# Gate and up of a SwiGLU FFN as one stage in emission order: where the sums of x, the first unit's preparation and the last unit's products stand

## The chip, the cores and the metric

The kernel runs on one core of one Trainium2 chip. The metric is the device time of one execution in microseconds (us). A core has five engines with a queue of instructions each: TensorE (PE) for matmuls, with its weight loads shown apart as PEld, VectorE (DVE), ScalarE (ACT), GpSimd (POOL) and SyncE (SP), which here only issues DMAs. An engine takes its instructions in the order of its queue; between engines, semaphores hold an instruction until its inputs are there and its output's memory is free.

## The reference

One decoder block on x of 512 tokens by 1024 features, in float32: a half FFN, a mixer (retention and a convolution, gated), and another half FFN, each with a residual and a layer norm behind it. The change touches only the gate and up products of the two FFNs.

```python
def swiglu_ffn(h, w_gate, w_up, w_down):
    return (jax.nn.silu(h @ w_gate) * (h @ w_up)) @ w_down

    for l in range(DEPTH):
        x = layer_norm(alpha * x + 0.5 * swiglu_ffn(x, ffn1_w_gate[l], ffn1_w_up[l], ffn1_w_down[l]), ...)
        m = hybrid_mixer(x, ...)
        x = layer_norm(alpha * x + m, ln2_g[l], ln2_b[l])
        x = layer_norm(alpha * x + 0.5 * swiglu_ffn(x, ffn2_w_gate[l], ffn2_w_up[l], ffn2_w_down[l]), ...)
```

w_gate and w_up are 1024 x 2816, w_down is 2816 x 1024.

## The kernel before

**Numbers in two parts.** Every operand of a matmul is split into a rounded part and a rest (`split`: a cast on ACT writes the "hi" tile, a subtraction on DVE writes the "lo" tile), and each product is three matmuls: hi·hi, hi·lo, lo·hi. `xh` and `xl` are the two parts of x, features on the partitions.

**Units.** The 2816 columns of gate and up are 22 units of 128 columns (`NF`). A unit is one DMA of 1 MB into a `raw` tile (two buffers), holding the unit's gate and up weights. The first `N_STD` units (2 in FFN1, 3 in FFN2) are done plainly: `feat_proj` for gate and for up, 24 matmuls of 512 columns each, then `silu_times`: silu of gate on ACT (tile `sg`), times up on DVE, into `h`. In FFN1 the first of them is `first_unit`, which loads the weights and x in pieces; in FFN2 two are started by the mixer's last layer norm (`token_proj` with `ahead`), their weight parts lying in tiles `z` of the mixer's pool "mix". The last of the plain units is called the late unit below; it goes through `load_unit`.

**Strassen units.** The other units (20 in FFN1, 19 in FFN2) compute gate and up of one unit as a 2 x 2 block product by a Strassen-Winograd scheme with seven products in place of eight. For x, `strassen_x` forms four sums once for each FFN: f3 = b12 - b22, f1 = b11 - b12, f2 = -f1 - b22, f4 = f2 + b21 (each 128 x 1024), and splits them into `th`, `tl` (called t3, t1, t2, t4). In FFN2 x exists only as xh and xl, so each term is two operations. For each unit, `strassen_w` gives named steps: `load` (DMA), `s13` (one DVE operation), `s24` (two, of which the second reads the first), four casts on ACT (`hi_a` for a12 and a11, `hi_b` for s1 and s3, `hi_c` for s2 and s4, `hi_d` for a22) and four subtractions on DVE (`lo_a` to `lo_d`).

**The loop** is `strassen_rows`, in a section (`tc.manual_schedule()`) in which each engine's queue keeps the order in which the code emits it. Everything outside of such a section is ordered by a scheduler. A product is 12 matmuls of 256 columns. The order of PE in iteration u is: a11·b11 into bank z; s3·t3 into bank y; the s4·b22 of the unit before, into its z; s2·t2 added to z; a12·b21 into bank w; a22·t4 added to y; s1·t1 added to z. Since banks are added to, copies are taken by ACT (`z1`, `y1`, `z2`) before the next product goes into the same bank; `g1` = z1 + w is gate's first half, z after s4·b22 its second half; the two halves of up are `row2` = y - z2 and y1 - z. The next unit's steps are laid between these with `do(...)`. For the last unit the loop runs one iteration more, in which only s4·b22 and the outputs are left.

**Before the loop**, the sums of x, the splits, the silus of the plain units and the first Strassen unit's steps are outside of the section, so the scheduler places them.

**Memory.** Pools are stacked. In before, `th`, `tl` and `sg` are in pool "gu", the sums (`tf`, and `xf`, x as loaded in FFN1) in a pool "xin" above it, closed before the loop, and the loop's tiles in pool "strassen", which takes the place of "xin". A pool that takes the place of closed ones waits for their last users; with `reuse_waits="tile"` each tile waits only for those that lay at its own addresses.

Of the kernel before, what the change touches and what calls it, by code (L numbers as in the profile page):

```python
# [52 lines left out]
def block_kernel(ctx, tc, ap, out):  # L53
# [48 lines left out]
    def strassen_x(pool, tmp, parts):  # L102

        b = {}
        for i in range(2):
            for j in range(2):
                sl = (slice(None), slice(i * KH, (i + 1) * KH), slice(j * HS, (j + 1) * HS))
                b[i, j] = [p[sl] for p in parts], (xh[sl], xl[sl])

        def total(first, *rest):  # L110

            f = tmp.tile([P, KH, HS], F32, name="tf", bufs=2)
            terms = [(p, op) for ps, op in rest for p in ps]
            acc = first
            for p, op in terms:
                nc.vector.tensor_tensor(f, acc, p, op=op)  # L116
                acc = f
            return f

        def pair(f):  # L120
            hi = pool.tile([P, KH, HS], F32R, name="th", bufs=4)
            lo = pool.tile([P, KH, HS], F32R, name="tl", bufs=4)
            split(hi, lo, f)
            return hi, lo

        (b11, b12, b21, b22) = (b[i][0] for i in ((0, 0), (0, 1), (1, 0), (1, 1)))
        f3 = total(b12[0], (b12[1:], ALU.add), (b22, ALU.subtract))
        t3 = pair(f3)
        f1 = total(b11[0], (b11[1:], ALU.add), (b12, ALU.subtract))
        t1 = pair(f1)  # L130
        f2 = tmp.tile([P, KH, HS], F32, name="tf", bufs=2)
        nc.vector.scalar_tensor_tensor(f2, f1, -1.0, b22[0], op0=ALU.mult, op1=ALU.subtract)
        for p in b22[1:]:
            nc.vector.tensor_tensor(f2, f2, p, op=ALU.subtract)
        t2 = pair(f2)
        f4 = total(f2, (b21, ALU.add))
        return {"b11": b[0, 0][1], "b21": b[1, 0][1], "b22": b[1, 1][1],
                "t1": t1, "t2": t2, "t3": t3, "t4": pair(f4)}

    def strassen_w(pool, src):  # L140
# [15 lines left out]
        def s13():  # L156
            s[13] = pool.tile([P, 2, 512], F32, name="s13")
            nc.vector.tensor_tensor(s[13], raw[:, 0:4:2], raw[:, 3:4].to_broadcast([P, 2, 512]), op=ALU.add)  # L158

        def s24():  # L160
            s[24] = pool.tile([P, 2, 512], F32, name="s24")
            nc.vector.tensor_tensor(s[24][:, 0], s[13][:, 0], raw[:, 2], op=ALU.add)
            nc.vector.tensor_tensor(s[24][:, 1], s[24][:, 0], raw[:, 1], op=ALU.add)
# [18 lines left out]
    def strassen_rows(pool, units, xs, row1_done, row2_done, unit_done):  # L182
# [19 lines left out]
        prep = strassen_w(pool, units[0])  # L202
        for step in ("load", "s13", "hi_a", "hi_b", "s24", "lo_a", "hi_c", "lo_b", "hi_d", "lo_c", "lo_d"):
            prep[step]()
        with tc.manual_schedule():
            prev = None
            for u in range(len(units) + 1):
                n = strassen_w(pool, units[u + 1]) if u + 1 < len(units) else None

                def do(*steps):  # L210
                    for step in steps:
                        if n:
                            n[step]()

                do("load")
                cur = None
                if u < len(units):
                    w = prep["w"]
                    cur = dict(z=bank()[:, :HS], y=bank()[:, :HS], w=bank()[:, :HS], ws=w)
                    product(cur["z"], w["a11"], xs["b11"], True)  # L220
                if prev:
                    prev["row2"] = row2_done(u - 1)
                    nc.vector.tensor_tensor(prev["row2"][:, HS:], prev["y1"], prev["z"], op=ALU.subtract)
                do("hi_a", "s13")
                if cur:
                    z1 = copy("z1", cur["z"])
                    product(cur["y"], w["s3"], xs["t3"], True)
                do("hi_b", "lo_a")
                if cur:
                    cur["y1"] = copy("y1", cur["y"])  # L230
                if prev:
                    product(prev["z"], prev["ws"]["s4"], xs["b22"], False)
                    row1_done(u - 1, 1, prev["z"])
                do("s24", "lo_b", "hi_c")
                if prev:

                    nc.vector.tensor_tensor(prev["row2"][:, :HS], prev["yd"], prev["z2"], op=ALU.subtract)
                    unit_done(u - 1)
                if cur:
                    product(cur["z"], w["s2"], xs["t2"], False)  # L240
                    cur["z2"] = copy("z2", cur["z"])
                do("hi_d", "lo_c")
                if cur:
                    product(cur["w"], w["a12"], xs["b21"], True)
                    g = small("g1")
                    nc.vector.tensor_tensor(g, z1, cur["w"], op=ALU.add)
                    row1_done(u, 0, g)
                do("lo_d")
                if cur:
                    product(cur["y"], w["a22"], xs["t4"], False)  # L250
                    cur["yd"] = cur["y"]
                    product(cur["z"], w["s1"], xs["t1"], False)
                prev, prep = cur, n
# [209 lines left out]
    def ffn(w_gu, w_dn, res, row, dst, n_std, begin, ahead):  # L463
        with ExitStack() as es:
# [6 lines left out]
            with ExitStack() as es2:  # L471
                gp = es2.enter_context(tc.tile_pool(name="gu", bufs=1))

                def silu_times(ft, ps):
                    sg = gp.tile([P, S], F32, name="sg", bufs=2)
                    nc.scalar.activation(sg, ps[0], AF.Silu)
                    nc.vector.tensor_tensor(h[ft], ps[1], sg, op=ALU.mult)

                with tc.tile_pool(name="xin", bufs=1) as xp:
                    started, parts = begin(xp)  # L480
                    for ft in range(len(started)):
                        silu_times(ft, started[ft])
                    late = [unit_proj(w_gu[ft]) for ft in range(len(started), n_std)]
                    xs = strassen_x(gp, xp, parts)
                    for ft in range(len(started), n_std):
                        silu_times(ft, late[ft - len(started)])
                sp = es2.enter_context(tc.tile_pool(name="strassen", bufs=1, reuse_waits="tile"))
                sgs, ups = {}, {}

                def gate(u, half, src):  # L490
                    if half == 0:
                        sgs[u] = gp.tile([P, S], F32, name="sg", bufs=2)
                    nc.scalar.activation(sgs[u][:, half * HS:(half + 1) * HS], src, AF.Silu)

                def up(u):
                    ups[u] = sp.tile([P, S], F32, name="up2", bufs=2)
# [5 lines left out]
                strassen_rows(sp, [w_gu[ft] for ft in range(n_std, NF)], xs, gate, up, both)  # L502
# [18 lines left out]
    def first_unit(gp):  # L521
# [4 lines left out]
        xf = gp.tile([P, KD, S], F32, name="xf")  # L526
# [6 lines left out]
        def first_x(k):  # L533
            nc.sync.dma_start(xf[:, k, :], ap["xT"][:, k, :])
            split(xh[:, k, :], xl[:, k, :], xf[:, k, :])
# [12 lines left out]
        return [ps0], [xf]  # L548

    w_in = ap["w_in"]  # L550
    qk_glu = ffn(ap["w1gu"], ap["w1dn"], ap["x"], 0, scratch1, N_STD[0], first_unit, (w_in[U_QK], w_in[U_L]))
# [271 lines left out]
    def started_units(gp):  # L823
        return started, [xh.bitcast(F32), xl.bitcast(F32)]

    ffn(ap["w2gu"], ap["w2dn"], scratch2, 4, out, N_STD[1], started_units, ())
# [84 lines left out]
```

## Time and profile before

| | us |
|---|---|
| median of 3 runs | 1401.92 |
| lowest and highest | 1400.29, 1402.74 |
| the profiled execution, its own time | 1402.5 |
| its span, from first to last instruction | 1400.1 |
| PE busy | 1377.9 |
| DVE busy | 992.3 |
| ACT busy | 598.3 |

The span is what the profiler sees of one execution; the execution's own time is 2.4 us longer. Times in the rows below are from the span's start. A matmul's busy time overlaps the next one's, so a pace is read from the starts. In a row, "L191" is line 191 of the kernel, "out<-in" its tiles by name, and a bracket at the end is the idle time before it and what ended it.

### The profile page before, as it was taken

How to read it: one execution, taken by the hardware profiler on the slowest of the kernel's cores; microseconds unless marked ns; L12 is line 12 of the kernel's file. 1: busy time of each engine (PE TensorE's matmuls, PEld its weight loads, DVE VectorE, ACT ScalarE, POOL GpSimd, SP SyncE). 2: the span in 40 equal slices, each digit the busy share in tenths (PEclk: the TensorE clock that was granted, in tenths of full speed). 3: DMA queues.
4: the chain of work that ended last, by engine and by line, in shares of the span. 5: the costliest groups of instructions: out<-in, count | busy, mean ns of one | idle time of the engine just before them, and what ended most of it. 6: DMA issues, size and time to landing. Idle time of an engine off the chain costs nothing.

```text
span 1400.1 us, 19305 instructions
## 1 busy us (share of the span) xinstructions
PE 1377.9 (98%) x7974; PEld 1219.1 (87%) x7974; DVE 992.3 (71%) x1410; ACT 598.3 (43%) x872; POOL 21.8 (2%) x36
## 2 busy tenths in 40 slices
PE   8999999999999999999999999999998999999997
PEld 6999999888988888888888888888887999998886
DVE  7878786335787786786788996645497787884336
ACT  6545554233434434445344422473234555553221
POOL 0000000000000000000000000000000000000000
PEclk9999999999999999999999999999998999999999
DMA  5332234324322232231222223222340323235221
GB/s 188 119 110 102 103 109 159 143 91 154 147 75 98 73 107 84 90 106 69 90 98 91 91 91 151 85 96 91 133 169 30 120 93 115 96 108 194 90 90 60
DMA packets 26006, 150.83 MB, mean 108 GB/s; under 512 B 2880, under 2 KB 3008, under 8 KB 10432
## 3 DMA queue, kind: packets, MB, share of 16 engines
q1 hardware_dynamic: 25920, 149.62, 29.7%
q8 instruction: 62, 1.02, 0.3%
q14 instruction: 24, 0.20, 0.0%
HBM read 143.32 MB, written 6.29 MB: 107 GB/s over the span
## 4 chain that ended last, share of the span: by engine, by line
PE 94%; DVE 4%; DMA 1%; ACT 1%; issue 1%; POOL 0%; SPq 0%; DVEq 0%; ACTq 0%
PE ps L191 28%; PE ps L400 19%; PE ps L259 13%; PE ps L260 13%; PE ps L258 13%; PE ps L618 2%; PE ps L619 2%; PE ps L620 2%; DMA xf<-in_xT_dram 1%; DVE tl L66 1%; PE ps L706 0%; DVE ln_y L369 0%; PE ps L381 0%; DVE tf L116 0%; DVE s L158 0%
## 5 line engine op out<-in xcount | busy, mean ns | idle before, releaser
L65 ACT CAST whi<-raw 128x1024 fp32r<-128x1024 f32 x156 | 162.8, 1050 | 266.9 <-PE ps L259 162.8
L66 DVE TENSOR_TENSOR wlo<-raw,whi 128x1024 fp32r<-128x1024 f32 x156 | 190.2, 1222 | 73.2 <-ACT whi L65 72.4
L258 PE MATMUL ps<-xh,whi 128*128 128x512 f32 x512 | 200.8, 392 | 1.2 <-ACT whi L65 1.2
L260 PE MATMUL ps<-xh,wlo 128*128 128x512 f32 x512 | 200.2, 391 | 0.7 <-DVE wlo L66 0.7
L259 PE MATMUL ps<-xl,whi 128*128 128x512 f32 x512 | 200.0, 391 | 0.0
L291 DVE SCALAR_TENSOR_TENSOR cv<-up,vec,cv 128x512 f32<-128x512 f32 x240 | 179.4, 748 | 4.2
L260 PEld LDWEIGHTS ps<-xh,wlo 128*128 128x128 f32 x512 | 96.5, 189 | 21.4 <-DVE wlo L66 1.2
L258 PEld LDWEIGHTS ps<-xh,whi 128*128 128x128 f32 x512 | 96.6, 189 | 21.0 <-ACT whi L65 1.6
L259 PEld LDWEIGHTS ps<-xl,whi 128*128 128x128 f32 x512 | 96.5, 188 | 19.5
L400 PE MATMUL ps<-whi,hh 128*128 128x512 f32 x352 | 110.1, 390 | 2.0 <-ACT hh L65 2.0
L400 PE MATMUL ps<-whi,hl 128*128 128x512 f32 x352 | 109.8, 389 | 0.0
L400 PE MATMUL ps<-wlo,hh 128*128 128x512 f32 x352 | 109.7, 389 | 0.0
L66 DVE TENSOR_TENSOR hl<-h,hh 128x512 fp32r<-128x512 f32 x44 | 29.7, 690 | 110.1 <-ACT hh L65 110.1
L191 PE MATMUL ps<-th,whi 128*128 128x256 f32 x312 | 89.0, 285 | 4.0 <-ACT whi L148 4.0
L191 PE MATMUL ps<-th,wlo 128*128 128x256 f32 x312 | 89.0, 285 | 0.5 <-DVE wlo L151 0.5
L191 PE MATMUL ps<-tl,whi 128*128 128x256 f32 x312 | 88.8, 285 | 0.0
L191 PE MATMUL ps<-xh,whi 128*128 128x256 f32 x312 | 88.5, 284 | 0.0
L191 PE MATMUL ps<-xl,whi 128*128 128x256 f32 x312 | 88.4, 283 | 0.0
L191 PE MATMUL ps<-xh,wlo 128*128 128x256 f32 x312 | 88.4, 283 | 0.0
L65 ACT CAST hh<-h 128x512 fp32r<-128x512 f32 x44 | 26.6, 623 | 130.4 <-PE ps L400 130.4
L400 PEld LDWEIGHTS ps<-whi,hh 128*128 128x128 f32 x352 | 65.8, 188 | 15.9 <-ACT hh L65 2.4
L400 PEld LDWEIGHTS ps<-whi,hl 128*128 128x128 f32 x352 | 66.1, 188 | 13.8
(211 smaller groups left out, 3284.8 us busy)
## 6 DMA issues: line engine op xcount, KB each, us to landing
raw<-in_w_in_dram SPq DMA_DIRECT2D x40, 1024.0 KB, 4.9
raw<-in_w2gu_dram SPq DMA_DIRECT2D x22, 1024.0 KB, 4.8
raw<-in_w1gu_dram SPq DMA_DIRECT2D x21, 1024.0 KB, 4.9
raw<-in_w1dn_dram SPq DMA_DIRECT2D x11, 1024.0 KB, 4.9
raw<-in_w2dn_dram SPq DMA_DIRECT2D x11, 1024.0 KB, 4.8
raw<-in_w_ret_dram SPq DMA_DIRECT2D x8, 1024.0 KB, 4.9
ln_r<-scratch SPq DMA_DIRECT2D x8, 512.0 KB, 8.2
raw<-in_w_conv_dram SPq DMA_DIRECT2D x4, 1024.0 KB, 4.8
```

Of the source, the lines that this page charges most:

```text
L65: nc.scalar.copy(hi, src)
L66: nc.vector.tensor_tensor(lo, src, hi.bitcast(F32), op=ALU.subtract)
L191: mm(ps, a[:, sl], c[:, k, :], start=(first and k == 0 and n == 0), stop=(k == KH - 1 and n == 2), skip_group_check=True)
L258: mm(ps, wh[wsl], xh[xsl], start=first, stop=False)
L259: mm(ps, wh[wsl], xl[xsl], start=False, stop=False)
L260: mm(ps, wl[wsl], xh[xsl], start=False, stop=last)
L291: op = nc.vector.scalar_tensor_tensor(c, up[:, t:t + S], vcol(C_CK + i * TAPS + t), c, op0=ALU.mult, op1=ALU.add)
L400: mm(acc[st][hf], x[:, sl], wx[:, hf * 512:(hf + 1) * 512], start=(k == 0 and x is ah and wi == 0), stop=(k == nk - 1 and x is al),)
L618: mm(o, xh[:, k, ssl], wh[:, csl], start=(k == 0), stop=False)
L619: mm(o, xh[:, k, ssl], wl[:, csl], start=False, stop=False)
L620: mm(o, xl[:, k, ssl], wh[:, csl], start=False, stop=(k == KD - 1))
```

## The change

The stage from the first gate product to the last unit's output becomes one section in emission order. `strassen_x` no longer computes; it returns named steps f1 to f4, hi1 to hi4 (cast on ACT), lo1 to lo4 (subtraction on DVE). `ffn` lays them among the first Strassen unit's steps in a written order, with the silus between, all ahead of the loop. The x of FFN1 (`xf`) now lies in eight of the `h` tiles, so a sum there is formed in four operations of 256 columns. The sums and s13, s24 share one tile name, `st`, with three buffers. Pools "xin" and "strassen" are gone; all is in "gu". `z1`, `y1`, `z2` and `g1` have one buffer each, not two. The `row2` half y - z2 is taken at the end of its own unit. The last unit's order is s1·t1, a22·t4, s4·b22, and the extra iteration is gone.

```diff
-    def strassen_x(pool, tmp, parts):
...
+    def strassen_x(pool, parts):
...
+        def form(t, scale, first, plus, minus):
+
+            def step():
+                out = pool.tile([P, KH, HS], F32, name="st", bufs=3)
+                for n, (ks, terms) in enumerate(parts(*(plus or minus if t in ("t2", "t4") else first))):
+                    o = out[:, ks]
...
+                    for p, op in ts:
+                        if scale != 1.0 and acc is not o:
+                            nc.vector.scalar_tensor_tensor(o, acc, scale, p, op0=ALU.mult, op1=op)
+                        else:
+                            nc.vector.tensor_tensor(o, acc, p, op=op)
+                        acc = o
+                f[t] = out
+            return step
+
+        def pair(t):
+            def hi():
+                xs[t] = (pool.tile([P, KH, HS], F32R, name="th", bufs=4), pool.tile([P, KH, HS], F32R, name="tl", bufs=4))
+                nc.scalar.copy(xs[t][0], f[t])
+
+            def lo():
+                nc.vector.tensor_tensor(xs[t][1], f[t], xs[t][0].bitcast(F32), op=ALU.subtract)
             return hi, lo
...
         def s13():
-            s[13] = pool.tile([P, 2, 512], F32, name="s13")
+            s[13] = pool.tile([P, 2, 512], F32, name="st", bufs=3)
...
-            return pool.tile([P, HS], F32, name=name, bufs=2)
+            return pool.tile([P, HS], F32, name=name)
...
+        prev = None
+        for u in range(len(units)):
+            last = u == len(units) - 1
...
+            do("load")
+            w = prep["w"]
+            cur = dict(z=bank()[:, :HS], y=bank()[:, :HS], w=bank()[:, :HS], ws=w, row2=row2_done(u))
+            product(cur["z"], w["a11"], xs["b11"], True)
+            if prev:
+                row2(prev, 1)
+            do("hi_a", "s13")
+            z1 = copy("z1", cur["z"])
+            product(cur["y"], w["s3"], xs["t3"], True)
+            do("hi_b", "lo_a")
+            cur["y1"] = copy("y1", cur["y"])
+            if prev:
+                product(prev["z"], prev["ws"]["s4"], xs["b22"], False)
+                row1_done(u - 1, 1, prev["z"])
+            do("s24", "lo_b", "hi_c")
+            if prev:
+                unit_done(u - 1)
+            product(cur["z"], w["s2"], xs["t2"], False)
+            cur["z2"] = copy("z2", cur["z"])
+            do("hi_d", "lo_c")
+            product(cur["w"], w["a12"], xs["b21"], True)
+            g = small("g1")
+            nc.vector.tensor_tensor(g, z1, cur["w"], op=ALU.add)
+            row1_done(u, 0, g)
+            do("lo_d")
+            if last:
+                product(cur["z"], w["s1"], xs["t1"], False)
+                row2(cur, 1)
+                product(cur["y"], w["a22"], xs["t4"], False)
+                row2(cur, 0)
+                product(cur["z"], w["s4"], xs["b22"], False)
+                row1_done(u, 1, cur["z"])
+                unit_done(u)
+            else:
+                product(cur["y"], w["a22"], xs["t4"], False)
+                row2(cur, 0)
+                product(cur["z"], w["s1"], xs["t1"], False)
+            prev, prep = cur, n
...
+            with tc.tile_pool(name="gu", bufs=1) as gp, tc.manual_schedule():
+                xs, x_steps = strassen_x(gp, begin_parts(h))
+                prep = strassen_w(gp, w_gu[n_std])
+                steps = prep | x_steps
+                ps = begin(h)
+                n_begun = len(ps)
+                late = [load_unit(w_gu[ft]) for ft in range(n_begun, n_std)]
+                for ws in late:
+                    ps.append([bank(), bank()])
+                    for j in range(2):
+                        feat_proj(ps[-1][j], ws[j])
...
+                do("load s13 hi_a f3 hi_b hi3 lo_a lo3 lo_b s24 hi_c f1 hi1 lo_c f2")
+                silu_times(0)
+                do("lo1 hi2 lo2 f4 hi_d hi4")
+                if n_begun > 1:
+                    silu_times(1)
+                do("lo_d lo4")
+                for ft in range(n_begun, n_std):
+                    silu_times(ft)
...
-                sp = es2.enter_context(tc.tile_pool(name="strassen", bufs=1, reuse_waits="tile"))
...
+    def first_parts(h):
+
+        xf = h[NF - KD:]
+        return lambda i, j: [(k, [xf[i * KH + k][:, j * HS:(j + 1) * HS]]) for k in range(KH)]
...
-        xf = gp.tile([P, KD, S], F32, name="xf")
+        xf = h[NF - KD:]
...
+    def split_parts(h):
+        def parts(i, j):
+            sl = (slice(None), slice(i * KH, (i + 1) * KH), slice(j * HS, (j + 1) * HS))
+            return [(slice(0, KH), [p.bitcast(F32)[sl] for p in (xh, xl)])]
```

## Rows read from the trace of the kernel before

**Rows 1.** The page: busy us of an engine (share of the span), instructions.

```profile
PE 1377.9 (98%) x7974; PEld 1219.1 (87%) x7974; DVE 992.3 (71%) x1410; ACT 598.3 (43%) x872; POOL 21.8 (2%) x36
```

**Rows 2.** Windows: stretch, us, busy us (instructions) by engine, PE's granted clock, DMA, GB/s.

```profile
21.70:25.30 3.60, 3.60 (x11) 2.81 (x10) 3.57 (x4) 1.82 (x2) 0.00 (x0) 0.53 0.51 155
...
43.40:234.50 191.10, 191.09 (x1593) 190.88 (x1591) 152.90 (x205) 98.89 (x170) 0.00 (x0) 1.00 0.31 111
...
1075.00:1083.20 8.20, 6.66 (x27) 6.07 (x28) 8.13 (x10) 4.97 (x8) 0.00 (x0) 0.50 0.39 128
```

**Rows 3.** Waits of PE over the span: total us, times, longest us.

```profile
PE ps L191 <- ACT whi L148: 4.0, 1, 4.0
```

**Rows 4.** Timeline of PE: the starts of both loops; start us, us long, instruction.

```profile
18.18 0.39 PE L260 MATMUL ps<-xh,w 128*128 128x512 f32 x1
...
42.81 0.28 PE L191 MATMUL ps<-xh,whi 128*128 128x256 f32 x1
...
1069.42 0.28 PE L191 MATMUL ps<-xh,whi 128*128 128x256 f32 x1
...
1074.99 0.58 PE L191 MATMUL ps<-th,whi 128*128 128x256 f32 x1 [3.98 <-ACT whi L148]
...
1087.22 0.28 PE L191 MATMUL ps<-xh,whi 128*128 128x256 f32 x1
```

**Rows 5.** Timeline of PE: the last unit of FFN1.

```profile
234.21 0.28 PE L191 MATMUL ps<-th,wlo 128*128 128x256 f32 x1
235.00 0.39 PE L191 MATMUL ps<-xh,chi 128*128 128x256 f32 x1 [0.52 <-DVE up L223]
```

**Rows 6.** Timeline of DVE: a unit of FFN1's loop, and FFN2's sums.

```profile
53.09 0.42 DVE L223 TENSOR_TENSOR up<-y,ps 128x256 f32<-128x256 f32 x1 [1.73 <-PE ps L191]
53.43 1.22 DVE L158 TENSOR_TENSOR s<-raw 128x1024 f32<-128x1024 f32 x1
54.56 1.22 DVE L151 TENSOR_TENSOR wlo<-raw,whi 128x1024 fp32r<-128x1024 f32 x1
...
58.68 0.69 DVE L500 TENSOR_TENSOR h<-up,sg 128x512 f32<-128x512 f32 x1
59.29 1.22 DVE L151 TENSOR_TENSOR clo<-s,chi 128x1024 fp32r<-128x1024 f32 x1
...
1046.83 2.36 DVE L116 TENSOR_TENSOR tf<-xh,xl 128x1024 f32<-128x1024 f32 x2 [0.24 <-DMA scratch<-ln_y]
...
1064.38 1.22 DVE L132 SCALAR_TENSOR_TENSOR tf<-tf,xh 128x1024 f32<-128x1024 f32 x1
1065.63 1.22 DVE L134 TENSOR_TENSOR tf<-tf,xl 128x1024 f32<-128x1024 f32 x1
```

**Rows 7.** Timeline of ACT: the start of FFN2's loop.

```profile
1058.75 1.28 ACT L476 ACT_TABLE_LOAD   x1 [13.70 <-PE ps L260]
1060.05 1.09 ACT L476 ACTIVATE sg<-ps 128x512 f32<-128x512 f32 x2
1061.02 2.01 ACT L65 CAST th<-tf 128x1024 fp32r<-128x1024 f32 x2
...
1085.06 0.42 ACT L493 ACTIVATE sg<-g 128x256 f32<-128x256 f32 x1 [1.36 <-DVE g L246]
```

**Rows 8.** Groups of ACT by shape, loop of FFN1: busy us, mean ns | idle before.

```profile
L199 ACT COPY z<-ps 128x256 f32<-128x256 f32 x38 | 14.2, 373 | 45.4 <-PE ps L191 45.2
```

**Rows 9.** Two lines' DMA issues in FFN1's start: issue ns, start us; landing us.

```profile
L75 SPq DMA_DIRECT2D raw<-in_w1gu_dram x1: 328/328/328, 8.9 to 8.9; - x1
...
DMA to landing us min/median/max: 8.2/8.2/8.2
...
L154 SPq DMA_DIRECT2D raw<-in_w1gu_dram x1: 328/328/328, 13.4 to 13.4; - x1
...
DMA to landing us min/median/max: 6.2/6.2/6.2
```

**Rows 10.** Timeline of POOL behind FFN1: five tiles of pool "mix".

```profile
385.39 0.35 POOL L585 MEMSET up<- 128x30 f32 x5 [18.45 <-PE ps L260]
```

More of the change, by code (lines that the diff above doesn't have):

```diff
@@ L93, in load_ahead @@
         return parts[:2], parts[2:]
-    def strassen_x(pool, tmp, parts):
[L104 to L123, printed above, removed]
-            return hi, lo
[L126 to L138, printed above, removed]
@@ new lines, in strassen_x @@
+    def strassen_x(pool, parts):
+        xs, f = {}, {}
+        for name, i, j in (("b11", 0, 0), ("b21", 1, 0), ("b22", 1, 1)):
+            sl = (slice(None), slice(i * KH, (i + 1) * KH), slice(j * HS, (j + 1) * HS))
+            xs[name] = xh[sl], xl[sl]
+        def form(t, scale, first, plus, minus):
[3 more added lines that the diff above has]
+                    o = out[:, ks]
+                    ts = [(p, ALU.add) for p in parts(*plus)[n][1]] if plus else []
+                    ts += [(p, ALU.subtract) for p in parts(*minus)[n][1]] if minus else []
+                    if t in ("t1", "t3"):
+                        ts = [(p, ALU.add) for p in terms[1:]] + ts
+                        acc = terms[0]
+                    else:
+                        acc = f[first][:, ks]
+                    for p, op in ts:
[12 more added lines that the diff above has]
+                nc.vector.tensor_tensor(xs[t][1], f[t], xs[t][0].bitcast(F32), op=ALU.subtract)
+            return hi, lo
+        steps = {"f3": form("t3", 1.0, (0, 1), None, (1, 1)), "f1": form("t1", 1.0, (0, 0), None, (0, 1)),
+                 "f2": form("t2", -1.0, "t1", None, (1, 1)), "f4": form("t4", 1.0, "t2", (1, 0), None)}
+        for n in "1234":
+            steps["hi" + n], steps["lo" + n] = pair("t" + n)
+        return xs, steps
@@ L156, in s13 @@
         def s13():
-            s[13] = pool.tile([P, 2, 512], F32, name="s13")
+            s[13] = pool.tile([P, 2, 512], F32, name="st", bufs=3)
             nc.vector.tensor_tensor(s[13], raw[:, 0:4:2], raw[:, 3:4].to_broadcast([P, 2, 512]), op=ALU.add)
         def s24():
-            s[24] = pool.tile([P, 2, 512], F32, name="s24")
+            s[24] = pool.tile([P, 2, 512], F32, name="st", bufs=3)
             nc.vector.tensor_tensor(s[24][:, 0], s[13][:, 0], raw[:, 2], op=ALU.add)
@@ L180, in strassen_w, with strassen_rows @@
                     lo_a=lambda: lo["a"](), lo_b=lambda: lo["b"](), lo_c=lambda: lo["c"](), lo_d=lambda: lo["d"]())
-    def strassen_rows(pool, units, xs, row1_done, row2_done, unit_done):
+    def strassen_rows(pool, units, prep, xs, row1_done, row2_done, unit_done):
         def product(ps, w, x, first):
@@ L200, in copy @@
             return t
[L202 to L253, printed above, removed]
@@ new lines, in strassen_rows, with do, row2 @@
+        prev = None
+        for u in range(len(units)):
+            last = u == len(units) - 1
+            n = strassen_w(pool, units[u + 1]) if not last else None
+            def do(*steps):
+                for step in steps:
+                    if n:
+                        n[step]()
+            def row2(c, half):
+                sl = slice(half * HS, (half + 1) * HS)
+                a, b = ((c["y"], c["z2"]), (c["y1"], c["z"]))[half]
+                nc.vector.tensor_tensor(c["row2"][:, sl], a, b, op=ALU.subtract)
+            do("load")
[31 more added lines that the diff above has]
+                unit_done(u)
+            else:
+                product(cur["y"], w["a22"], xs["t4"], False)
+                row2(cur, 0)
+                product(cur["z"], w["s1"], xs["t1"], False)
+            prev, prep = cur, n
@@ L460, in unit_rows, with ffn @@
         return get
-    def ffn(w_gu, w_dn, res, row, dst, n_std, begin, ahead):
+    def ffn(w_gu, w_dn, res, row, dst, n_std, begin, begin_parts, ahead):
         with ExitStack() as es:
@@ L470, in ffn, with silu_times, do @@
             h = [spare_h([P, S], F32) for ft in range(NF)]
-            with ExitStack() as es2:
-                gp = es2.enter_context(tc.tile_pool(name="gu", bufs=1))
-                def silu_times(ft, ps):
-                    sg = gp.tile([P, S], F32, name="sg", bufs=2)
[L476 to L486, printed above, removed]
-                sp = es2.enter_context(tc.tile_pool(name="strassen", bufs=1, reuse_waits="tile"))
+            with tc.tile_pool(name="gu", bufs=1) as gp, tc.manual_schedule():
[9 more added lines that the diff above has]
+                        feat_proj(ps[-1][j], ws[j])
+                def silu_times(ft):
+                    sg = gp.tile([P, S], F32, name="sg", bufs=2)
+                    nc.scalar.activation(sg, ps[ft][0], AF.Silu)
+                    nc.vector.tensor_tensor(h[ft], ps[ft][1], sg, op=ALU.mult)
+                def do(names):
+                    for name in names.split():
+                        steps[name]()
+                do("load s13 hi_a f3 hi_b hi3 lo_a lo3 lo_b s24 hi_c f1 hi1 lo_c f2")
[6 more added lines that the diff above has]
+                    silu_times(ft)
                 sgs, ups = {}, {}
@@ L495, in up @@
                 def up(u):
-                    ups[u] = sp.tile([P, S], F32, name="up2", bufs=2)
+                    ups[u] = gp.tile([P, S], F32, name="up2", bufs=2)
                     return ups[u]
@@ L500, in both @@
                     nc.vector.tensor_tensor(h[n_std + u], ups[u], sgs[u], op=ALU.mult)
-                strassen_rows(sp, [w_gu[ft] for ft in range(n_std, NF)], xs, gate, up, both)
+                strassen_rows(gp, [w_gu[ft] for ft in range(n_std, NF)], prep, xs, gate, up, both)
             dp = es.enter_context(tc.tile_pool(name="dn", bufs=1, reuse_waits="tile"))
@@ L533, in first_x @@
         def first_x(k):
[L534 to L535 removed]
+            nc.sync.dma_start(xf[k], ap["xT"][:, k, :])
+            split(xh[:, k, :], xl[:, k, :], xf[k])
         for hf in range(2):
```

12 lines of the change are left out of this document (6 added, 6 removed).

## The prediction

> **What bounds the kernel now.** I read the busy shares first. TensorE (PE) is busy for 98% of the span [rows 1], so only time in which PE stands, or runs at its lower clock, can change the end. The windows come next: the unit loop of the first FFN runs 1593 matmuls in 191.1 us, 0.12 us each, with PE never idle and the granted clock at 1.00, while DVE is busy 152.9 us and ACT 98.9 us of it [rows 2]. That loop can't gain from this change; its edges can. [...] The waits of PE name the longest: 4.0 us, in the second FFN, for a weight half-cast on ACT [rows 3]. The timeline of PE gives the marks that I count from [rows 4]. In FFN1 the standard units' matmuls pause after 18.18 and the second Strassen unit starts at 42.81. In FFN2 the first Strassen unit starts at 1069.42, stands until 1074.99, and the second unit starts at 1087.22. Last, the end of each loop: the last unit's product with s4 starts 0.79 us after the matmul before it, where 0.12 is the pace, waiting for the DVE read of the same bank [rows 5]; the second FFN's end has the same wait.
>
> **What the change fixes: the order of ACT and DVE.** In before, a section in emission order shows what such an order costs: DVE stands 1.73 us for z ahead of s13, which is the next unit's work and reads only weights [rows 6], and ACT stands 1.36 us ahead of a silu [rows 7]. Nothing overtakes. Now the sums of x, the first unit's preparation and the silus are inside that section, *ahead* of the unit loop. The loop's first unit needs three ACT copies: z1 before the s2·t2 product may add into bank z, y1 before a22·t4, z2 before s1·t1. In the new ACT queue, z1 stands behind hi4, the late silus and hi_a of the second unit; y1 stands behind hi_b of that unit, and z2 behind its hi_c. And hi4 needs f4, the last of the chain of sums on DVE. So PE waits for nearly all of the preparation, not only for the tiles that it multiplies.
>
> **Prices.** DVE, start to start [rows 6]: 1.13 us for a 1024-wide operation, 1.25 if the next one reads its result (so 0.12 more), 0.61 for 512 wide, 0.34 for 256 wide; s24, two of 512 with a read between them, 1.34. ACT [rows 7]: wide cast 1.05 (0.96 start to start), silu 0.6 (0.5 start to start), table load 1.28; copy of 256 columns 0.37 [rows 8].
>
> FFN1 forms its sums from eight separate tiles, so each of the four is four 256-wide operations, not one wide one: 4 × 0.34 = 1.36 against 1.13, 0.9 us more of DVE in all. [...]
>
> **FFN1.** The late unit's weights land at 8.9 + 8.2 = 17.1 and the first Strassen unit's at 13.4 + 6.2 = 19.6 [rows 9]. Casts of the late unit follow from 17.1, its two wlo free DVE at 20.55. The DVE queue from there: s13 1.13, f3 1.36, lo_a 1.13, lo3 1.25 (waits for hi3), lo_b 1.13, s24 1.34, f1 1.36, lo_c 1.13, f2 1.36, h of the first unit 1.31 (it waits 0.7 for the silu, behind hi1 and the table load), lo1 and lo2 2.26, f4 1.44 to its end: 16.2, so f4 is there at 36.75. ACT then: hi4 1.05, silu 0.5, hi_a 0.96, z1 0.37: 39.6. PE resumes with the late unit at 18.4, waits for its wlo until 19.5, and 46 matmuls of 0.23 us (512 columns, twice the 0.12), a11 and s3 (2.88) bring it to 32.9. So it stands some 6.7 us, and whatever it gained on the late unit is swallowed. Four products of 1.44 us are left in the unit, 5.8 us. After such a stand I take the low clock for 3.4 us, about the length of the window at 21.7 [rows 2], which costs half of it, 1.7. The second unit starts at 39.6 + 5.8 + 1.7 = 47.1 against 42.81: **+4.3 us**.
>
> [...]
>
> **FFN2.** Here a second thing bites. All tiles of the stage now come from the pool gu, which lies partly where the mixer's pool with the started units' weights (tile z) lay. In before its first tile, sg, is held until PE's last read of z: ACT stands 13.70 us to 1058.75 [rows 7]. Is that by pool or by tile? After FFN1 five memsets of five up buffers all start at 385.39, in the moment PE leaves the old pool [rows 10]; five addresses with one release speak for the pool. In before the sums had a pool of their own elsewhere and started at 1046.83, nearly 12 us earlier [rows 6]. So s13, now the first gu tile and first in the section's DVE queue, starts at 1058.75, and everything behind it too. From there: s13 1.13, f3 3.63 (three wide ones, chained), lo_a 1.13, lo3 1.27, lo_b 1.13, s24 1.34, f1 3.63, lo_c 1.13, f2 2.38, h 0.61, lo1 and lo2 2.26, f4 2.5: 22.1, so 1080.9. ACT: hi4 1.05, two silus 1.0, hi_a 0.96, z1 0.37: 1084.3. PE is through s3 at 1069.42 + 2.88 = 1072.3 and stands 12 us. But z2 comes later still: DVE waits for the second silu to 1082.6, then h 0.61, lo_d 0.61, lo4 1.13, h 0.61, s13 1.13, lo_a 1.13, s24 1.41, that is 1089.2; hi_c 1.05 and z2 0.37 put s1·t1 at 1090.65 and the second unit at 1092.1 against 1087.22: **+4.9 us**. The three products between fit into the 6.3 us even with 3.4 us of low clock.
>
> **The last unit.** With s1·t1 first, the DVE read of z lies under the 1.44 us of a22·t4. The gap of 0.79 shrinks to 0.12, 0.67 us in each FFN: **-1.3 us**. The stage's end is as before: silu, then the first hh cast.
>
> **The rest at nothing.** The row2 half moved to the end of its unit and the single z1, y1, z2, g1 buffers: DVE's 1.73 us of idle time per unit [rows 6] covers 0.34; each buffer's reader is done most of a unit before the next write, and a late one would cost its lateness in every unit. The three st buffers are reused behind reads that stand earlier in the same queues. SP issues the same loads in the same order; the third unit's load waits for lo_d (1083.9 in FFN2) and with the 6.2 us of [rows 9] lands at 1090, ahead of its first use near 1092; with the 8.2 us it would be level. If it were late, hi_a and the copies behind it would be late by as much.
>
> **Sum:** 4.3 + 4.9 - 1.3 = +7.9, of which I take 7.6, since each chain rounds its waits up. The profiled execution took 1402.5 us (span 1400.1), 0.6 above the median of 1401.92; on the median that is 1409.5.
>
> **Rivals.**
> *The low clock lasts longer.* In FFN2 it lasted 8.2 us [rows 2]. Then FFN1 loses up to 4.1 instead of 1.7 and FFN2 some 1.4 more: +3.8, 1413.3. Against it: the window of FFN1, 3.6 us.
> *The copies don't wait behind the preparation.* If the queue let them ahead, DVE would still be late: its read of z for the first unit would end at 47.2 and 1093.1, where PE wanted the bank at 45.7 and 1090.1 (second unit plus 2.88): +1.5 + 3.0 - 1.3 = +3.2, 1405.1. Against it: the orders in [rows 6, 7].
> *Faster: the pool doesn't hold s13.* If st tiles wait only for what lay at their own addresses, s13 starts at 1046.7 behind the layer norm's last DVE work. The chain then ends at 1068.8, z1 is in time, y1 and z2 cost about 1 us each, and the second unit starts at 1080.1: -7.1 in FFN2. With +4.3 and -1.3 that is -4.1, 1397.8. Each microsecond that s13 starts earlier saves about one, so it turns the sign once s13 starts before about 1051. Against it: the five memsets.
> *The change does little:* the new order comes out like the scheduler's old one, and only the last unit gains: -1.3, 1400.6. For it: the same operations on the same engines; against it, z1 behind hi4.
>
> **Chances.** Forecast 0.70, longer low clock 0.08, copies ahead 0.08, pool doesn't hold 0.09, little 0.05. The range takes in the first three: 1404.0 (1405.1 less a microsecond for its rounding) to 1413.5. What a measurement can tell here is about 0.2%, 2.8 us. Slower by more: the first two and most of the third, 0.83; within: 0.08; faster: 0.09.
>
> **What would show it.** ACT: z1 of the first unit directly behind hi_a of the second, near 39.2 and 1084. PE: in each FFN one stand ahead of the first matmul into z with chi, some 6 and 12 us, released by an ACT copy; a low clock behind it. DVE: s13 of FFN2 at 1058.8, released by PE. No wait for up at the loops' ends. I am wrong if s13 starts near 1047, or if z1 stands ahead of hi4.

## The result and the profile after

The changed kernel takes 1409.14 us, the median of 4 runs (1408.32 to 1410.10), beside 1401.32 of the kernel before (1400.29 to 1402.74, also 4). The ratio is 1.0055, with a 95% interval of 1.0038 to 1.0073: slower by 7.8 us, where +7.6 was forecast. The profiled execution took 1410.1 us with a span of 1408.2, 8.1 above the span of before.

The busy shares of the page, which answer to [rows 1]:

```profile
PE 1376.9 (98%) x7974; PEld 1219.9 (87%) x7974; DVE 996.5 (71%) x1422; ACT 598.2 (42%) x872; POOL 21.8 (2%) x36
```

The same matmuls keep PE busy about as long as before (1376.9 us, 1377.9 before); DVE has 4.2 us more. No engine has 8 us more to do, so the loss is time in which PE stands. The waits of PE over the span (total us, times, longest), beside [rows 3]:

```profile
PE ps L199 <- ACT z L207: 18.0, 2, 11.7
PE ps L410 <- ACT hh L65: 2.0, 2, 1.0
```

The 4.0 us for whi are gone. In their place PE waits twice, once in each FFN and 18.0 us in all, for an ACT copy of bank z. The timeline of PE, at the marks of [rows 4]: the first Strassen unit, the wait, and the start of the second unit, for FFN1 and then FFN2.

```profile
30.29 0.28 PE L199 MATMUL ps<-xh,whi 128*128 128x256 f32 x1
...
39.59 0.58 PE L199 MATMUL ps<-th,chi 128*128 128x256 f32 x1 [6.27 <-ACT z L207]
...
47.63 0.28 PE L199 MATMUL ps<-xh,whi 128*128 128x256 f32 x1
...
1073.43 0.28 PE L199 MATMUL ps<-xh,whi 128*128 128x256 f32 x1
...
1088.18 0.58 PE L199 MATMUL ps<-th,chi 128*128 128x256 f32 x1 [11.72 <-ACT z L207]
...
1094.50 0.39 PE L199 MATMUL ps<-th,whi 128*128 128x256 f32 x1
...
1096.04 0.28 PE L199 MATMUL ps<-xh,whi 128*128 128x256 f32 x1
```

Both waits stand ahead of s2·t2, the first matmul with chi. FFN1's second unit starts at 47.63 against 42.81, 4.82 later. FFN2's starts 22.61 us behind the first one (1096.04 - 1073.43) against 17.80 before [rows 4], 4.81 later. The timeline of ACT shows what the copy stood behind, in FFN1 and in FFN2:

```profile
36.79 1.04 ACT L135 CAST th<-st 128x1024 fp32r<-128x1024 f32 x1 [2.92 <-DVE st L127]
37.74 0.59 ACT L495 ACTIVATE sg<-ps 128x512 f32<-128x512 f32 x1
38.23 1.04 ACT L155 CAST whi<-raw 128x1024 fp32r<-128x1024 f32 x1
39.16 0.38 ACT L207 COPY z<-ps 128x256 f32<-128x256 f32 x1
...
1077.15 1.28 ACT L495 ACT_TABLE_LOAD   x1
1078.45 0.60 ACT L495 ACTIVATE sg<-ps 128x512 f32<-128x512 f32 x1
...
1084.90 1.04 ACT L135 CAST th<-st 128x1024 fp32r<-128x1024 f32 x1 [3.70 <-DVE st L127]
1085.85 1.08 ACT L495 ACTIVATE sg<-ps 128x512 f32<-128x512 f32 x2
1086.81 1.04 ACT L155 CAST whi<-raw 128x1024 fp32r<-128x1024 f32 x1
1087.75 0.38 ACT L207 COPY z<-ps 128x256 f32<-128x256 f32 x1
```

That is hi4, the late silus, hi_a of the second unit, z1, in this order, and hi4 itself waits for the last sum, f4. The timeline of DVE has f4 in FFN1, and in FFN2 the start of the chain, which answers to the sums in [rows 6]; below it, from the timeline of PE, the last matmul that reads the mixer's z:

```profile
35.33 1.43 DVE L127 TENSOR_TENSOR st<-st,h 128x256 f32<-128x256 f32 x4
36.66 0.69 DVE L158 TENSOR_TENSOR dlo<-raw,dhi 128x512 fp32r<-128x512 f32 x1
...
1062.73 1.22 DVE L165 TENSOR_TENSOR st<-raw 128x1024 f32<-128x1024 f32 x1 [12.95 <-PE ps L270]
```

```profile
1062.40 0.29 PE L270 MATMUL ps<-xh,z 128*128 128x256 f32 x1
```

In FFN2 DVE stands 12.95 us ahead of s13, until PE's last read of the mixer's z. The windows, beside [rows 2]: behind either wait the granted clock is at 0.50 and a matmul starts every 0.21 us (39.97 to 44.23 and 1088.57 to 1092.41 in the timeline of PE); inside the loop the clock is at 1.00 and the pace is still 0.12 us a matmul, without a stand.

```profile
39.59:44.45 4.86, 4.86 (x23) 4.86 (x23) 4.83 (x7) 2.45 (x4) 0.00 (x0) 0.50 0.40 167
...
1088.18:1092.40 4.22, 4.21 (x19) 4.22 (x20) 4.19 (x5) 1.32 (x2) 0.00 (x0) 0.50 0.71 248
...
48.00:235.00 187.00, 187.00 (x1561) 187.00 (x1560) 152.85 (x202) 96.94 (x166) 0.00 (x0) 1.00 0.31 111
```

Last, FFN1's final product in the timeline of PE, beside [rows 5]:

```profile
239.03 0.29 PE L199 MATMUL ps<-th,dlo 128*128 128x256 f32 x1
239.15 0.28 PE L199 MATMUL ps<-xh,chi 128*128 128x256 f32 x1
...
241.72 0.73 PE L410 MATMUL ps<-whi,hh 128*128 128x512 f32 x2 [0.98 <-ACT hh L65]
```

The product with s4 follows at the pace, 0.12 us, where it stood 0.79. From the second unit to the first matmul of the down product (L410) it is 194.09 us (241.72 - 47.63); in before, where that matmul starts at 237.68, 194.87. So FFN1's end gives back 0.78, and so does FFN2's (184.01 us from its second unit, where before has 184.79). The parts add up: 4.82 + 4.81 - 2 × 0.78 = 8.07, the 8.1 of the spans. The traced execution is the slowest of the four.

### The profile page after: what moved, and what is told of

Read it like the earlier page. It is cut to its first block, busy times and chain, and to the rows that moved or that the text cites. A ratio compares the mean times of both kernels' runs of the same rounds, so it can differ in the third digit from the quotient of the medians.

```text
span 1408.2 us, 19281 instructions
## 1 busy us (share of the span) xinstructions
PE 1376.9 (98%) x7974; PEld 1219.9 (87%) x7974; DVE 996.5 (71%) x1422; ACT 598.2 (42%) x872; POOL 21.8 (2%) x36
## 4 chain that ended last, share of the span: by engine, by line
PE 92%; DVE 5%; DMA 2%; ACT 1%; issue 0%; SPq 0%; POOL 0%; DVEq 0%; POOLq 0%
PE ps L199 28%; PE ps L410 18%; PE ps L269 13%; PE ps L270 13%; PE ps L268 13%; PE ps L645 2%; PE ps L647 2%; PE ps L646 2%; DVE st L127 1%; DMA raw<-in_w_in_dram 1%; DMA raw<-in_w1gu_dram 1%; PE ps L733 0%; DVE tl L138 0%; DMA h<-in_xT_dram 0%; DVE ln_y L379 0%
## 5 line engine op out<-in xcount | busy, mean ns | idle before, releaser
L410 PE MATMUL ps<-whi,hh 128*128 128x512 f32 x352 | 110.2, 390 | 2.0 <-ACT hh L65 2.0
L410 PE MATMUL ps<-wlo,hh 128*128 128x512 f32 x352 | 109.8, 390 | 0.0
L410 PE MATMUL ps<-whi,hl 128*128 128x512 f32 x352 | 109.8, 389 | 0.0
L410 PEld LDWEIGHTS ps<-whi,hh 128*128 128x128 f32 x352 | 65.9, 188 | 15.8 <-ACT hh L65 2.4
L410 PEld LDWEIGHTS ps<-wlo,hh 128*128 128x128 f32 x352 | 66.1, 188 | 13.7
```

Source lines behind the costliest of these rows:

```text
L410: mm(acc[st][hf], x[:, sl], wx[:, hf * 512:(hf + 1) * 512], start=(k == 0 and x is ah and wi == 0), stop=(k == nk - 1 and x is al),)
```

## The experiments

The theory: the copies stand in ACT's queue behind preparation that they don't need, and pool gu holds that preparation back in FFN2. The main rivals: DVE has too much to do whatever the order, or the release isn't the pool's. All times, with the kernel before run beside each on the same chip:

| run | median us | before us | ratio (95%) |
|---|---|---|---|
| e1 last unit's order alone | 1401.04 | 1402.79 | 0.9988 (0.9979 to 0.9997) |
| e2 copies ahead | 1404.99 | 1402.79 | 1.0020 (1.0011 to 1.0029) |
| e3 sums in another pool | 1404.39 | 1402.79 | 1.0013 (1.0005 to 1.0022) |
| e4 both of these | 1399.80 | 1402.79 | 0.9980 (0.9971 to 0.9989) |
| e6 release by tile | 1404.54 | 1402.97 | 1.0012 (1.0002 to 1.0021) |
| e7 two sums first in FFN1 | 1408.24 | 1402.97 | 1.0043 (1.0031 to 1.0056) |
| e5 order rewritten | 1390.28 | 1402.97 | 0.9913 (0.9900 to 0.9927) |
| e8 rewritten, copies ahead | 1389.35 | 1402.95 | 0.9906 (0.9890 to 0.9923) |

To place a gain, two marks from each timeline of PE: where the first s4·b22 starts in FFN1, and in FFN2 how far it starts behind the first Strassen matmul (in before 1090.10 - 1069.42).

| | before | after | e1 | e2 | e3 | e4 | e6 | e7 | e5 | e8 |
|---|---|---|---|---|---|---|---|---|---|---|
| FFN1 | 45.69 | 50.51 | 46.58 | 47.42 | 48.66 | 47.16 | 49.43 | 48.68 | 44.56 | 42.84 |
| FFN2 | 20.68 | 25.49 | 20.97 | 23.66 | 20.63 | 18.74 | 21.01 | 25.47 | 11.58 | 11.51 |

The FFN1 mark moves by itself: after, e3 and e6 have the same order there and lie within 1.9 us, and before and e1, which share an order too, 0.9 apart. A single difference below that says nothing. The shifts of both marks and 1.56 us for the ends give each span to 0.3 us, save for e2 (3.2 against 5.7 above before) and e4 (-2.0 against -0.9): there the clock fell behind a mark as well (to 0.50 in the 3 us behind 47.42 in e2, last section; in e4 a matmul starts only every 0.21 us behind 47.16).

**e1, the last unit's order alone**, in the kernel before (`if last:` in its loop, the extra iteration dropped):

```diff
+                if last:
+                    row2 = row2_done(u)
+                    product(cur["z"], w["s1"], xs["t1"], False)
+                    nc.vector.tensor_tensor(row2[:, HS:], cur["y1"], cur["z"], op=ALU.subtract)
+                    product(cur["y"], w["a22"], xs["t4"], False)
...
+                    product(cur["z"], w["s4"], xs["b22"], False)
```

> The kernel before with one part of the change alone: the last unit's products in the order s1·t1, a22·t4, s4·b22, without the extra iteration. Theory: it gains the two gaps of 0.79 us down to the pace of 0.12, and the short ramp of the first matmul after each, 0.8 us per FFN: -1.6 us, 1399.7, with no wait of PE for up left. Rival (the change's loss comes from this order too): 1401.3 or more.

Measured: -1.7 us; the interval just excludes no change. The timeline of PE at FFN1's last unit:

```profile
235.10 0.28 PE L191 MATMUL ps<-th,dlo 128*128 128x256 f32 x1
235.22 0.32 PE L191 MATMUL ps<-xh,chi 128*128 128x256 f32 x1
```

The stand is gone here too, so the order of the last unit gives this gain without the rest of the change.

**e2, the copies ahead.** In the changed kernel the first Strassen unit's a11 and s3 products and the copies z1 and y1 are emitted behind hi2, ahead of the rest of the preparation; s2·t2 and z2 come ahead of the second unit's s13.

```diff
+        def early():
+            product(begun["z"], prep["w"]["a11"], xs["b11"], True)
+            begun["z1"] = copy("z1", begun["z"])
+            product(begun["y"], prep["w"]["s3"], xs["t3"], True)
+            begun["y1"] = copy("y1", begun["y"])
...
+                do("lo1 hi2")
+                next(rows)()
+                do("lo2 f4 hi_d hi4")
```

> The changed kernel, with the first unit's a11 and s3 products and their copies z1 and y1 emitted right behind hi2, and z2 ahead of the second unit's s13 and hi_b; the DVE order is kept. Theory (PE stands because the copies queue on ACT behind the preparation; what stays is DVE's lateness): FFN1's first s2·t2 starts near 35.5 with lo2 instead of 39.6, and the bound moves to the DVE read of z for the second unit's s4·b22, near 47.2 against 50.5 in the changed kernel; in FFN2 near 1097.1 against 1098.9. Gain -3.3 and -1.8 against the changed kernel: 1404.0. Rival (the amount of DVE work ahead of the loop costs the time, wherever the copies stand): no change, 1409.1.

Measured: +2.2 us against before, so 5.6 of the 7.8 are gone. Waits of PE over the span:

```profile
PE ps L199 <- ACT z L207: 5.0, 2, 4.5
PE ps L199 <- DVE tl L138: 4.2, 4, 1.4
PE ps L199 <- DVE up L233: 2.7, 2, 1.3
```

The wait for z falls from 18.0 to 5.0 us by moving instructions alone, so their place in the queue was the cause. The 4.5 us that are left stand in FFN2, where the copies are still behind hi2 and with it behind the held chain. Another part returns as waits for DVE, which is late with lo2, lo4 and the first unit's outputs: the rival that the prediction priced at 1405.1. The traced execution, at 1407.66, is the slowest of its eleven.

**e3, the sums in another pool.** The tiles st alone move to a pool of their own, above gu.

```diff
-                out = pool.tile([P, KH, HS], F32, name="st", bufs=3)
+                out = sums.tile([P, KH, HS], F32, name="st", bufs=3)
...
-            with tc.tile_pool(name="gu", bufs=1) as gp, tc.manual_schedule():
+            with tc.tile_pool(name="gu", bufs=1) as gp, tc.tile_pool(name="sums", bufs=1) as up_, tc.manual_schedule():
```

> The changed kernel with the tile st (the sums of x, s13, s24) in a pool of its own above gu, where the layer norm's tiles lay and not the mixer's; the order of all queues is kept. Theory (the hold of s13 by the pool until PE's last read of z starts the chain late): s13 and f3 run near 1051, the chain goes on with hi3 when gu is free at 1062.7, so lo3 starts at 1063.9 in place of 1068.7 and everything behind it in FFN2 is 4.8 us earlier; FFN1 as it is: 1404.3. Rival (the hold is by tile, or the chain isn't what PE waits for): s13 near 1062.7, 1409.1; or s13 early and the time the same.

Measured: +1.6. FFN2's mark, 20.63, is back at the 20.68 of before. The timelines of DVE and of ACT:

```profile
1048.61 1.23 DVE L165 TENSOR_TENSOR st<-raw 128x1024 f32<-128x1024 f32 x1 [0.73 <-DMA scratch<-ln_y]
...
1061.84 1.23 DVE L138 TENSOR_TENSOR tl<-st,th 128x1024 fp32r<-128x1024 f32 x1 [7.21 <-ACT th L135]
```

```profile
1060.76 1.05 ACT L135 CAST th<-st 128x1024 fp32r<-128x1024 f32 x1 [9.72 <-PE ps L270]
```

s13 no longer waits for PE, and starts 22.85 us ahead of the first Strassen matmul (at 1071.46), where it was 10.70 in after (1073.43 - 1062.73). But tile th is still in gu: its cast is held until PE's last read of z, and DVE stands 7.21 us for it at lo3. So of 12.2 us 4.9 arrive (25.49 - 20.63). Freeing one tile left the hold with the next.

**e4, both edits**, the diffs of e2 and of e3 in one kernel:

> The changed kernel with both edits, copies ahead and the sums in a pool of their own. Theory: FFN1 as with the copies ahead (-3.3); in FFN2 the chain is 4.8 us earlier, PE stands little after s3 and waits for the DVE read of z near 1092.2 against 1098.9 (-6.7): 1399.1, below the kernel before. Rival (both edits remove the same wait, so together they give no more than the larger one): 1404.

Measured: -3.0, a little better than expected. The two edits nearly add up: alone they took 5.6 and 6.2 us off the 7.8 that the change costs, together 10.8. All three carry the interval of that 7.8, which reaches from 5.3 to 10.2 us; FFN2's mark is steadier and says the same: 1.83 and 4.86 us earlier alone, 6.75 together.

**e6, release by tile.** One word in the changed kernel:

```diff
-            with tc.tile_pool(name="gu", bufs=1) as gp, tc.manual_schedule():
+            with tc.tile_pool(name="gu", bufs=1, reuse_waits="tile") as gp, tc.manual_schedule():
```

> The changed kernel with one word altered: pool gu releases by tile, each tile waiting only for those that lay at its own addresses, where the whole pool waited for all users of the closed ones. Theory (the hold on s13 in FFN2 is the pool's, and s13's own addresses are free sooner than the last z): s13 starts up to 10 us earlier against the first gate matmul, as in the run with the sums in another pool, and the time falls by 3 to 5 us against the changed kernel, to a ratio of about 1.002 to 1.003 against the kernel before. Rival (the addresses themselves are those of z that PE reads last, or PE's last read is what s13 needs in any case): s13 still starts behind PE's last read of z, and the time stays at a ratio of 1.005 to 1.006.

Measured: +1.6, the same as e3. The timelines of DVE and of ACT:

```profile
1054.53 1.23 DVE L165 TENSOR_TENSOR st<-raw 128x1024 f32<-128x1024 f32 x1 [5.81 <-PE ps L270]
```

```profile
1061.70 1.05 ACT L135 CAST th<-st 128x1024 fp32r<-128x1024 f32 x1 [4.86 <-PE ps L270]
```

s13 starts 17.84 us ahead of the first Strassen matmul (at 1072.37), against 10.70 in after. It still waits for a read of PE, which by the pool's rule is one of what lay at its own addresses, and th waits on until 1061.70. So the hold of the changed kernel is the pool's, as the five memsets had said [rows 10], and by tile part of it remains.

**e7, two sums first in FFN1.** f3 and f1 are formed in the 2.71 us in which DVE stood for the late unit's whi; hi1 and lo1 move up.

```diff
+                if n_begun == 1:
+                    steps["f3"]()
+                    steps["f1"]()
...
+                    do("load s13 hi_a hi_b hi3 hi1 lo_a lo3 lo_b lo1 s24 hi_c lo_c f2")
+                    silu_times(0)
+                    do("hi2 lo2 f4 hi_d hi4")
```

> The changed kernel with FFN1's order altered alone: f3 and f1 are formed ahead of the late unit's splits, where VectorE stood 2.7 us for whi, and hi1 and lo1 move up to stand behind hi3 and lo3. FFN2 as in the changed kernel. Theory (z1's copy stands on ScalarE behind hi4, and hi4 comes when f4 is formed at the end of VectorE's chain): the chain ends 2.7 us sooner, z1 is copied at about 36.5 instead of 39.2 us, PE stands 3.6 us instead of 6.27, and the time falls by 2.7 against the changed kernel, a ratio of about 1.0035 to 1.004 against the kernel before. Rival (VectorE's early idle time is of no use, since what it does at that place delays the late unit's lo parts and PE with them): PE's stand moves from z1 to the late unit's wlo at 19 to 22 us by as much, and the ratio stays at 1.0055.

Measured: ratio 1.0043, 0.0012 below after, with intervals that overlap. The time alone settles nothing: both forecast ratios lie within its interval. In the trace neither mechanism came out as forecast. The stand for wlo didn't grow (0.19 us, against 0.51 in after), and PE stood 5.74 us for z1 where the theory had 3.6; z1 came 8.35 us behind the first Strassen matmul, against 8.87. The timeline of DVE shows why so little arrived:

```profile
23.56 1.23 DVE L138 TENSOR_TENSOR tl<-st,th 128x1024 fp32r<-128x1024 f32 x1 [1.01 <-ACT th L135]
...
29.50 1.23 DVE L158 TENSOR_TENSOR clo<-st,chi 128x1024 fp32r<-128x1024 f32 x1 [1.11 <-ACT chi L155]
30.64 1.42 DVE L125 SCALAR_TENSOR_TENSOR st<-st,h 128x256 f32<-128x256 f32 x4
```

DVE now stands for ACT's casts further on (with two waits of 0.51 for th, 3.1 us in all), and f2, which starts the second half of the chain, comes at 30.64 as in after (30.49).

**e5, the order rewritten.** st, th and tl lie in a pool above gu, and the orders are:

```diff
+                if n_begun == 1:
+                    do("f3 f1")
...
+                if n_begun == 1:
+                    do("hi3 load s13 hi_a hi1 lo_a lo3 hi_b lo_b lo1 f2 hi2 s24 hi_c lo2 lo_c f4")
+                    silu_times(0)
+                    do("hi_d lo_d hi4 lo4")
...
+                    do("load hi_a lo_a f3 hi3 f1 hi1 lo3 f2 hi2 lo1 f4 hi4 lo2 lo4")
...
+                    do("s13 hi_b s24 lo_b hi_c lo_c hi_d lo_d")
```

> The changed kernel with two things altered. Tiles st, th and tl lie in a pool of their own, above gu, so that no sum waits for the mixer's z. And the written order ahead of the loop follows what each engine has free: in FFN1 f3 and f1 are formed ahead of the late unit's splits, the splits of x stand ahead of the first Strassen unit's hi_b and hi_c; in FFN2 x's sums and splits and two silus stand ahead of s13, and s13, s24 and the four splits of the unit come behind them. Theory (in-order queues and the pool's hold are all that the change cost): in FFN1 the first Strassen unit no longer stands, s4 x b22 comes at about 43.2 us where it was 45.69 in the kernel before, 2.5 less; in FFN2 the second Strassen unit begins 10.1 us behind the first (a unit's pace in the loop) where it was 17.8 in the kernel before, 7.7 less; the last units' order gives 1.6. Together 11.8 below the kernel before, about 0.84 per cent: ratio 0.9916. Rival (VectorE has too much to do here, whatever the order: its sums and splits set when products can start): as with both edits of the last batch, 3 below the kernel before, ratio 0.998, with PE's waits then on tl, wlo or up.

Measured: ratio 0.9913, 12.7 us below the kernel before. The timeline of PE, two waits and the start of the second unit in FFN1, then FFN2's first and second unit:

```profile
35.04 0.39 PE L199 MATMUL ps<-th,chi 128*128 128x256 f32 x1 [2.48 <-ACT z L207]
...
40.14 0.39 PE L199 MATMUL ps<-th,whi 128*128 128x256 f32 x1 [0.53 <-ACT z L207]
...
41.68 0.28 PE L199 MATMUL ps<-xh,whi 128*128 128x256 f32 x1
...
1067.71 0.28 PE L199 MATMUL ps<-xh,whi 128*128 128x256 f32 x1
...
1076.41 0.28 PE L199 MATMUL ps<-xh,whi 128*128 128x256 f32 x1
```

In FFN2 no stand is left: 8.70 us for six products of 1.44. The total came out as expected, its parts did not. FFN2 gave 9.10 where 7.7 were expected, because the first unit has no s4·b22 in it. FFN1 gave 1.13 where 2.5 were (45.69 - 44.56), a difference that the mark can't settle (against e1 it is 2.02); but the stand that was to go is there, 2.48 us, because z1 is still behind hi4, the silu and hi_a. The two make 11.8 with the 1.56 of the ends, and the spans differ by 11.7. A window over FFN1's start says what binds there now:

```profile
14.80:42.50 27.70, 24.30 (x142) 21.11 (x141) 27.57 (x42) 17.20 (x22) 0.00 (x0) 1.00 0.31 117
```

DVE, the third figure, is busy 27.57 of 27.70 us. How much of the gain is the pool's and how much the order's, e5 doesn't tell apart.

**e8, rewritten, with the copies of e2**, in FFN1 ahead of hi4:

```diff
-                    do("hi_d lo_d hi4 lo4")
+                    do("hi_d lo_d")
+                    next(rows)()
+                    do("hi4 lo4")
```

> The last kernel with the order rewritten, and with the first Strassen unit's a11 and s3 products and their copies z1 and y1 emitted ahead of what they don't need: in FFN1 ahead of hi4, in FFN2 behind the third silu as before; its s2 x t2 and z2 stand ahead of the second unit's s13. Theory (what FFN1 still stands for, 2.48 us for z1 and 0.53 us for z2, is the place of these copies in ScalarE's queue): z1 is copied near 32 us where it was 34.6, PE runs from s3 x t3 into s2 x t2 without a stand over half a microsecond, FFN1's second unit starts near 38.5 instead of 41.68 us, FFN2 is unchanged, and the time falls by 2.5 to 3.2 against that kernel, to 15 below the kernel before: ratio 0.989 to 0.990. Rival (behind the copies VectorE's splits are late by as much, as in the run that moved the copies alone, where PE then stood for tl and up): the stands move to tl, wlo or up, and the ratio stays at 0.991.

Measured: ratio 0.9906, some 1 us below e5 and not told from it by the intervals; 2.5 to 3.2 were expected. PE's waits for z in FFN1 are gone, and others have come, in the timeline of PE (the start of the second unit, and two waits in it):

```profile
37.67 0.28 PE L199 MATMUL ps<-xh,whi 128*128 128x256 f32 x1
...
40.04 0.39 PE L199 MATMUL ps<-th,wlo 128*128 128x256 f32 x1 [0.54 <-DVE wlo L158]
...
42.84 0.39 PE L199 MATMUL ps<-xh,chi 128*128 128x256 f32 x1 [1.34 <-DVE up L233]
```

The theory holds for the first unit: the second one starts 4.0 us earlier than in e5 (37.67 against 41.68), of which 0.5 is an earlier first Strassen matmul (29.00 against 29.52). The rival holds for what follows: with DVE full, PE waits 1.9 us for it within the second unit, and at s4·b22 1.7 us of the 4.0 are left (42.84 against 44.56). The order and the pool's hold account for the loss that the change brought, since the same operations run faster than before without them (e5). Whether a smaller part, as the narrower sums of FFN1, costs something beside them was not run. In FFN1 DVE's work is the next bound.

## Why the prediction was right

**In-order queues: right.** z1 stood where the prediction put it: PE resumed at 39.59 in FFN1, where 39.6 was forecast. In FFN2, with the shift of 4.01 from FFN1 taken off (1073.43 - 1069.42), z1 ended at 1084.12 (1087.75 + 0.38 - 4.01) against 1084.3, and s1·t1 started at 1090.49 (1094.50 - 4.01) against 1090.65. e2 shows that place was the cause.

**The hold by the pool: right.** s13 started at PE's last read of z, at 1062.73, 3.98 later than 1058.75, which is the shift of all of FFN2. e6 shows that the release was the pool's, e3 that another pool lifts it.

**FFN1, +4.3 forecast, +4.82 measured.** The mis-sized term is the low clock, taken for 3.4 us: it lasted 4.86, and the four products behind the stand took 8.04 us (47.63 - 39.59) where 7.5 were forecast. That size isn't fixed by the order of the instructions (last section), and the mark isn't either: by the traces with the order of after and with that of before, the change cost FFN1 between 2.1 us (48.66 - 46.58) and 4.8.

**FFN2, +4.9 forecast, +4.81 measured.** The low clock there (4.2 us) was covered: the product before s1·t1 starts at 1093.05 and takes 1.44, so it was done at 1094.49, when z2 had just been copied. The two limits came level, with no room left.

**The ends, -1.3 forecast, -1.56 measured.** The mis-sized term is the stand at 0.67 each: the way from the product behind it to L410 was also 0.11 us longer in before, as 237.68 - 235.00 = 2.68 against 241.72 - 239.15 = 2.57 says.

**The sum: closer than its accuracy.** The forecast parts make 7.9, the measured ones 8.07; the 0.3 us that was taken off for rounding answers to nothing in the trace. That 7.6 and 7.8 lie so close is in part luck: the interval of the 7.8 reaches from 5.3 to 10.2 us, and FFN1's mark alone moves by 1.9.

**The price of 0.34 us for a 256-wide operation held.** f4's four take 1.33 us from start to the next start (35.33 to 36.66), 0.33 each. The table load's 1.28 us held too: in FFN2 it runs from 1077.15 to 1078.43, and the silu starts at 1078.45, 0.02 us after its end.

**The rivals.** The one with the copies ahead was priced at +3.2 and e2 took +2.2; its marks are nearly exact (47.42 against the 47.2 forecast in FFN1; 1094.97, less the 1.89 by which e2's first FFN2 unit starts later, 1093.08 against 1093.1). But the price had no term for a clock that falls behind the stands for up, and in the traced execution it fell behind both, to 0.21 us a matmul from 47.80 and from 1095.31: that span is 5.7 us above the one of before, where the marks and the ends make 3.2. The faster rival was mispriced: with s13 free it gave FFN2 7.1 us below before. e3 gave 0.05, because th, held in the same pool, was left out of the step; e6, by addresses as the rival had it, started s13 7.1 us sooner against the first Strassen matmul than after did, and still left FFN2 0.33 above before (21.01 against 20.68).

## What to carry to other kernels

In a queue that keeps its order, emit a short copy that frees a PSUM bank (the memory that matmuls add into) ahead of all preparation that the waiting product doesn't need: here two copies of 0.38 us held PE for 6.3 and 11.7 us. When tiles move into a pool that takes the place of another one, ask for every tile which reader releases it: in e3, with one tile moved out, the wait stood at the next, 7.21 us. Write such an order from each engine's own timeline, a filled idle stretch being worth only what the next engine can take up: with the same operations, e5 took some 20 us off the changed kernel (1.0055 against 0.9913 of the kernel before), and e7, which only filled idle time, under 2.

## What the runs showed that was not expected

The granted clock does not follow from the length of one stand. In e5 PE stood 2.48 us and went on at a granted clock of 1.00. In the execution of e2 it stood 1.40 us for lo2 and went on at 1.00 from 35.61; later it stood 1.34 us for up and went on at 0.50 from 47.42. The windows, of e5 with the stand in it, and then of e2 behind either stand:

```profile
32.30:36.00 3.70, 1.22 (x11) 1.01 (x10) 3.70 (x5) 2.68 (x4) 0.00 (x0) 1.00 0.39 115
```

```profile
35.61:38.61 3.00, 3.00 (x24) 2.92 (x24) 2.48 (x6) 1.68 (x3) 0.00 (x0) 1.00 0.10 22
47.42:50.42 3.00, 3.00 (x14) 3.00 (x15) 2.96 (x4) 1.74 (x5) 0.00 (x0) 0.50 0.89 289
```

A longer stand left the clock up and a shorter one brought it down; what decides was not singled out by any run. And after the same stand of 6.3 us in FFN1 (6.27 in after, 6.28 in e3) the low level lasted 4.86 us in the one and no more than 3.3 in the other:

```profile
38.70:42.00 3.30, 3.30 (x17) 3.30 (x18) 3.27 (x5) 1.32 (x2) 0.00 (x0) 0.57 0.58 246
```

At 0.21 us a matmul, where 0.12 is the pace at 1.00, the 1.56 us between them cost some 0.7 us. So the price of a stand carries at least that much that differed between two executions with the same order there.
